# A planned two-layer decoder trunk: DeltaNet's gate projected with tokens as rows, memory accounted by single columns, the first gate bias loaded later

## The chip, the cores and the metric

The kernel runs on one core of a Trainium2 chip. The metric is the device time of one execution in microseconds, lower is better. Engines: PE (TensorE) with its weight loads PEld, DVE (VectorE), ACT (ScalarE), POOL (GpSimd), and SP, whose queue issues nearly all DMAs.

## What is computed

Two layers, each on x of 256 tokens by 1024 channels in fp32. One projection of the normalised x feeds three token mixers and three merge gates; the part that the change touches is the gate `za` of the first mixer, a gated delta rule with 4 heads of 128 (the reference, cut):

```python
def hybrid_layer(x, ...):
    h = rms_norm(x, norm_g)
    proj = jnp.einsum('btd,de->bte', h, w_in)
    (qa, ka, va, za, ba, aa, ub, zb, qc, kc, vc, zc, iq, ik, iw, gates) = split_columns(proj)
    ya = deltanet_branch(qa, ka, va, za, ba, aa, conv_w, a_log, dt_bias, dn_onorm)
    yb = pooling_branch(ub, zb, pool_w, pool_scale)
    yc = sparse_attention_branch(qc, kc, vc, zc, iq, ik, iw, ...)
    branches = jnp.stack([ya, yb, yc], axis=2)
    projected = jnp.einsum('btnc,ncd->btnd', branches, w_branch)
    gate = jax.nn.sigmoid(gates.reshape(b, t, N_BRANCH, D_MODEL) + gate_b)
    merged = jnp.sum(gate * projected, axis=2)
    return x + jnp.einsum('btd,de->bte', merged, w_out)

def deltanet_branch(...):
    ...
    o = chunk_gated_delta_rule(q, k, v, beta, g)
    o = rms_norm(o, o_norm) * jax.nn.silu(za.reshape(b, t, DN_HEADS, DN_DV))
    return o.reshape(b, t, DN_WIDTH)
```

## The kernel before

**Products.** Every large fp32 product is made of three matmuls on a rounded high part and the remainder as low part: high by high, high by low, low by high. A weight piece of 128 x 1024 comes by DMA into `raw` (4 buffers), ACT or DVE casts it to `wh` (6 buffers), and DVE subtracts to get `wl` (6 buffers); this is `wslot`. The activations are `hh` and `hl`, with channels on the partitions. `proj_cm` gives a result with channels as rows: for each block of 128 channels one weight piece, 24 matmuls of 256 columns (all tokens). `proj_tm` gives a result with tokens as rows: four weight pieces of 512 channels, held through two halves of 128 tokens, 24 matmuls of 512 columns each. PSUM banks are `pj` (4, projections) and `mx` (4, the rest).

**Scratch.** `u` (15 units of 512 columns), `f` (short-lived), `y` (fp32r operands of products), `big`, `tg` (merge gates and their biases), `z` (gates with channels as rows).

**The gate.** In DeltaNet's end the two token halves `o0`, `o1` are normalised, each is transposed by four PE transposes into an `mx` bank (`onT`), and these banks wait until `gated()`: it projects the gate with `zgate(ZA)` (two `proj_cm`, each followed by `silu2`, a tanh on ACT and one multiply on DVE), multiplies bank, scale `hb` and gate in one DVE instruction, and splits into `yah` and `yal`, the operands of the branch's output product.

**The order.** The program is written down once as a list of operations; the class `Plan` then orders them. `lay_out` is a list scheduler: it keeps a simulated time for each engine, holds operations that are ready, and picks by priority or by a deadline (`late`) that `deadlines` works out from the pass before; of 6 passes the best is kept. Its inputs are the prices in `cost`, `SWITCH` (what it charges PE for going from whole-array to small matmuls or back), the operations' earliest times `plan.begin`, and the dependences. These it finds from memory: `Ref.mask` gives the columns that an operand touches as a bit mask, in groups of four columns, and two operands with a common bit, one of them written, depend on each other. `emit` (L542) then issues everything in the order found, so every instruction in the profile has line L542, and rows are told apart by tile names. The order on each engine is fixed; the waits between engines are real.

**Stages, by time.** Load and normalise x, then k, v and the index projections of sparse attention (to about 57 us); its scores and top-k, DeltaNet's convolutions, the pooling mixer (57-190); the inverse of DeltaNet's triangular matrix in 32 x 32 blocks at 190, then its recurrence, the gate, branch products and output (190-320); the same for layer 1 (320-458, 458-576). The pooled channels go through a small product per group (`mx<-y,wl`), and k is transposed per head into `mx` banks, from which ACT takes sums of squares (`ssk`) and scaled copies.

Of the kernel before, what the change touches and what calls it, by code (L numbers as in the profile page):

```python
# [42 lines left out]
KOUT = 4  # L43
NWARM = 40

SWITCH = 90.0

REST = 2500.0

# [39 lines left out]
class Ref:  # L89
# [25 lines left out]
    def mask(self):  # L115
        (width, _), *free = self.ap.ap
        key = (self.ap.offset % width, tuple(free))
        got = self.tile.tag.masks.get(key)
        if got is None:
            idx = np.array([key[0]])  # L120
            for step, num in free:
                if step:
                    idx = (idx[:, None] + step * np.arange(num)[None, :]).reshape(-1)
            got = 0
            for g in np.unique(idx // 4):
                got |= 1 << int(g)
            self.tile.tag.masks[key] = got
        return got

# [54 lines left out]
class Plan:  # L184
# [35 lines left out]
    def cost(self, eng, call, args, kw):  # L220
# [28 lines left out]
            return hold + (120 if acc else 0), (95 if ps else 22) + (90 if acc else 0), False  # L249
        if eng == "POOL":  # L250
            if kw.get("op") == ALU.pow:
                return 400.0 + 155 * n, 240.0, False
            if call == "memset":
                return 50 + 0.8 * n, 50.0, False
            return 90 + 2.2 * w, 60.0, True
# [291 lines left out]
def trunk(ctx: ExitStack, tc: tile.TileContext, x, norm_g, w_in, gate_b, conv_w, a_log, dt_bias, dn_onorm,  # L547
# [32 lines left out]
    def unit(tag="u"):  # L580
        return make(tag, [128, 512])

    def fill():
        return make("f", [128, 512])
# [7 lines left out]
    def bank(tag):  # L592
        return plan.tile(tags[tag], [128, 512])

    def v4(t):
        return t.rearrange("p (h d) -> p h d", h=4)
# [123 lines left out]
    for l in range(DEPTH):  # L720
# [551 lines left out]
        V.tensor_tensor(o1, four(hsl(aT[1]), w1), qs, op=ALU.add)  # L1272


        onT = []
        for c, o in ((0, o0), (1, o1)):
            so, se, ro = small(4, "so"), small(4, "so2"), small(4, "so3")
            sumsq(o, so, unit())
            V.tensor_scalar(se, ssq[:, 4 * c:4 * c + 4], 4 * EPS, 128 * EPS, op0=ALU.add, op1=ALU.mult)
            V.scalar_tensor_tensor(se, so, 1.0 / 128, se, op0=ALU.mult, op1=ALU.add)  # L1280
            rsqrt(ro, se)
            V.tensor_tensor(v4(o), v4(o), ro[:, :, None].to_broadcast([128, 4, 128]), op=ALU.mult)
            ps = bank("mx")
            for h in range(4):
                PE.transpose(ps[:, h * 128:(h + 1) * 128], o[:, h * 128:(h + 1) * 128], ident)
            onT.append(ps)

        def gated():
            za = zgate(ZA)
            for c, ps in enumerate(onT):  # L1290
                y = unit()
                cc = slice(c * 128, (c + 1) * 128)
                V.scalar_tensor_tensor(v4(y), v4(ps), hb[:, 4:5], za[:, :, cc], op0=ALU.mult, op1=ALU.mult)
                split(v4(y), yah[:, :, cc], yal[:, :, cc])


        acc = [big()[:, :D] for _ in range(2)]
# [15 lines left out]
        for n, (i, yh, yl) in enumerate(((1, ybh, ybl), (2, ych, ycl), (0, yah, yal))):  # L1313
            wb = w_branch[l, i].rearrange("(k p) n -> p k n", p=128)
            gates = []
            if n == 2:
                gated()
            for half in range(2):
                cols = slice(half * 512, (half + 1) * 512)
                bias = make("tg", [128, 512], F32)  # L1320
                spread(DMA, bias, gate_b[l, i, cols])
                banks = by_token(wi[:, :, GT + i * D + half * 512:GT + i * D + (half + 1) * 512], KB, (hh, hl))
                tg = [make("tg", [128, 512], F32), bias]
                for t in range(2):
                    V.tensor_tensor(tg[t], banks[t], bias, op=ALU.add)
                    S.activation(tg[t], tg[t], AF.Tanh, scale=0.5)
                gates.append(tg)
            for half, tg in enumerate(gates):
                cols = slice(half * 512, (half + 1) * 512)
                banks = by_token(wb[:, :, cols], 4, (yh, yl))  # L1330
                for t in range(2):
                    at = acc[t][:, cols]
                    if n == 0:
                        V.scalar_tensor_tensor(at, tg[t], 1.0, banks[t], op0=ALU.add, op1=ALU.mult)
                        continue
                    V.scalar_tensor_tensor(tg[t], tg[t], 1.0, banks[t], op0=ALU.add, op1=ALU.mult)
                    V.tensor_tensor(at, at, tg[t], op=ALU.add)
                    if n == 2:
                        ps = bank("mx")
                        for k in range(4):  # L1340
                            c0 = half * 512 + k * 128
                            PE.transpose(ps[:, k * 128:(k + 1) * 128], acc[t][:, c0:c0 + 128], ident)
                        dst = [z[half][:, :, t * 128:(t + 1) * 128] for z in (mh, ml)]
                        S.activation(dst[0], v4(ps), AF.Copy, scale=0.5)
                        V.scalar_tensor_tensor(dst[1], v4(ps), 0.5, dst[0].bitcast(F32), op0=ALU.mult,
                                               op1=ALU.subtract)
# [63 lines left out]
```

## Time and profile before

| | us |
|---|---|
| median of 3 runs | 578.9 (578.34 to 580.63) |
| the profiled execution, its own time | 578.55 |
| its span, first to last instruction | 576.4 |
| PE busy | 566.5 |
| DVE busy | 484.8 |
| ACT busy | 297.0 |
| POOL busy | 35.6 |

The span is what the timelines cover; some 2 us of the execution lie outside it. An engine is busy while an instruction of its own runs; PE's matmuls are pipelined, so the pace is read from the distance between starts, not from the mean duration of one. In timelines a bracket gives the idle time before a row and the instruction that ended it.

### The profile page before, as it was taken

Reading aid. Unit: us, or ns where it says so; the run is one execution under the profiler, and the core shown is the slowest. Engines: PE = TensorE matmul, PEld = TensorE weight load, DVE = VectorE, ACT = ScalarE, POOL = GpSimd, SP = SyncE. Lnnn points to the kernel's source line nnn. Section 1 sums busy time; section 2 is a strip of 40 time slices with the busy share of each in tenths; the row PEclk is TensorE's granted clock in tenths of the full one; section 3 lists DMA queues with packets and bytes.
Section 4 is the critical chain, followed back from the end, with each engine's and each line's share of the span. In section 5 each row is a group of like instructions: output and inputs, shape, how many; then the busy total and the mean of one; then the engine's idle time right before and its main releaser. Section 6 shows DMA issues by size and latency. Waiting matters only on the chain.

```text
span 576.4 us, 10225 instructions
## 1 busy us (share of the span) xinstructions
PE 566.5 (98%) x3846; PEld 504.1 (87%) x3846; DVE 484.8 (84%) x1026; ACT 297.0 (52%) x574; POOL 35.6 (6%) x47
## 2 busy tenths in 40 slices
PE   8999999999999999999999999999999999999997
PEld 7887999998888789988879889999998878898886
DVE  5996999999999759658599999999999966766672
ACT  6754646756463452544346645776464534445520
POOL 4400000000100001000011002000100010000000
PEclk9999999999999999999999999999999999999999
DMA  9875458545766743565526559457457644666511
GB/s 309 266 209 163 112 145 235 134 144 167 228 182 211 202 129 110 183 216 186 181 64 215 148 140 257 112 150 202 137 160 231 205 141 113 178 193 207 177 38 73
DMA packets 95937, 98.71 MB, mean 171 GB/s; under 512 B 5616, under 2 KB 66848, under 8 KB 95888
## 3 DMA queue, kind: packets, MB, share of 16 engines
q1 hardware_dynamic: 95328, 97.47, 57.0%
q0 software_dynamic: 560, 0.60, 0.4%
q8 instruction: 30, 0.49, 0.4%
q14 instruction: 19, 0.16, 0.1%
HBM read 97.00 MB, written 1.05 MB: 170 GB/s over the span
## 4 chain that ended last, share of the span: by engine, by line
PE 82%; DVE 11%; issue 2%; ACT 2%; DMA 2%; POOL 1%; SPq 0%; DVEq 0%; ACTq 0%; POOLq 0%
PE pj L542 64%; PE mx L542 18%; DVE wl L542 4%; DVE u L542 3%; DVE big L542 1%; DMA x_sb<-in_x_dram 1%; DMA raw<-in_w_in_dram 1%; POOL r4k L542 1%; ACT u L542 1%; ACT wh L542 0%; DVE hl L542 0%; DVE y L542 0%; DVE tg L542 0%; POOL rk L542 0%; DVE wh L542 0%
## 5 line engine op out<-in xcount | busy, mean ns | idle before, releaser
L542 ACT CAST wh<-raw 128x1024 fp32r<-128x1024 f32 (+1 forms) x164 | 171.5, 1048 | 169.3 <-PE pj L542 117.8
L542 DVE TENSOR_TENSOR wl<-raw,wh 128x1024 fp32r<-128x1024 f32 (+1 forms) x174 | 211.1, 1220 | 32.4 <-ACT wh L542 26.8
L542 PE MATMUL pj<-wh,hh 128*128 128x512 f32 (+1 forms) x320 | 91.0, 388 | 0.9 <-ACT hh L542 0.9
L542 PE MATMUL pj<-wh,hl 128*128 128x512 f32 (+1 forms) x320 | 90.0, 386 | 1.1 <-DVE hl L542 1.1
L542 PE MATMUL pj<-wl,hh 128*128 128x512 f32 (+1 forms) x320 | 90.2, 385 | 0.0
L542 PEld LDWEIGHTS pj<-wh,hl 128*128 128x128 f32 x320 | 59.1, 188 | 13.0 <-DVE hl L542 2.0
L542 PEld LDWEIGHTS pj<-wh,hh 128*128 128x128 f32 x320 | 58.6, 188 | 11.9 <-ACT hh L542 1.3
L542 PEld LDWEIGHTS pj<-wl,hh 128*128 128x128 f32 x320 | 58.8, 188 | 10.7
L542 PE MATMUL pj<-hh,wh 128*128 128x256 f32 x448 | 64.4, 285 | 0.3 <-ACT wh L542 0.3
L542 PE MATMUL pj<-hl,wh 128*128 128x256 f32 x448 | 64.3, 284 | 0.0
L542 PE MATMUL pj<-hh,wl 128*128 128x256 f32 x448 | 63.6, 284 | 0.0
L542 PEld LDWEIGHTS pj<-hh,wh 128*128 128x128 f32 x448 | 58.3, 192 | 0.8 <-ACT wh L542 0.5
L542 PEld LDWEIGHTS pj<-hl,wh 128*128 128x128 f32 x448 | 58.1, 192 | 0.0
L542 PEld LDWEIGHTS pj<-hh,wl 128*128 128x128 f32 x448 | 58.0, 192 | 0.0
L542 PE MATMUL pj<-wh,y 128*128 128x512 f32 (+1 forms) x208 | 51.9, 384 | 0.0
L542 PEld LDWEIGHTS pj<-wh,y 128*128 128x128 f32 x208 | 38.3, 188 | 7.4
L542 PE MATMUL mx<-wh,y 128*128 128x512 f32 (+1 forms) x128 | 38.1, 380 | 0.0
L542 PEld LDWEIGHTS mx<-u,u 128*128 128x128 f32 (+2 forms) x336 | 31.2, 165 | 2.9 <-issue 2.1
L542 PE MATMUL mx<-u,u 128*128 128x128 f32 (+2 forms) x336 | 32.6, 249 | 0.0
L542 DVE SCALAR_TENSOR_TENSOR u<-pj,pt,u 128x255 f32<-128x255 f32 (+2 forms) x72 | 29.8, 480 | 0.0
L542 PE MATMUL pj<-wl,y 128*128 128x512 f32 (+1 forms) x104 | 29.2, 386 | 0.0
L542 PEld LDWEIGHTS mx<-wh,y 128*128 128x128 f32 x128 | 23.4, 188 | 4.4 <-DVE y L542 0.2
(206 smaller groups left out, 665.7 us busy)
## 6 DMA issues: line engine op xcount, KB each, us to landing
raw<-in_w_in_dram SPq DMA_DIRECT2D x128, 512.0 KB, 3.9
raw<-in_w_branch_dram SPq DMA_DIRECT2D x24, 512.0 KB, 3.4
raw<-in_w_out_dram SPq DMA_DIRECT2D x16, 512.0 KB, 3.3
tg<-in_gate_b_dram SPq DMA_DIRECT2D x12, 256.0 KB, 4.3
raw<-in_w_in_dram SPq DMA_DIRECT2D x4, 486.0 KB, 4.9
x_sb<-in_x_dram SPq DMA_DIRECT2D x2, 512.0 KB, 4.2
out_dram<-x_sb SPq DMA_DIRECT2D x3, 256.0 KB, 2.0
raw<-in_w_in_dram SPq DMA_DIRECT2D x2, 324.0 KB, 3.7
```

The lines of the kernel that those rows point to most:

```text
L542: getattr(self.real[o.eng], o.call)(*[put(a) for a in o.args], **{k: put(v) for k, v in o.kw.items()})
```

## The change

Five edits.

- The planner's price of a switch goes from 90 to 160 ns.
- `Ref.mask` marks single columns, not groups of four. Operands that lie in one group of four but share no column no longer depend on each other in the plan.
- The planner's price of POOL's power goes from 400 + 155n, with 240 until the result is seen, to 405 + 151n and 10.
- The DMAs of the gate biases may not be planned before 25 us (of the planner's time). This moves the first of them.
- DeltaNet's gate is projected by `proj_tm`. Each token half of `o` is multiplied by its gate while tokens are still rows, then transposed, and the scale `hb` is applied in two instructions that read the bank: ACT's copy makes the high part, one DVE instruction the low part.

```diff
-SWITCH = 90.0
+SWITCH = 160.0
...
-            got = 0
-            for g in np.unique(idx // 4):
-                got |= 1 << int(g)
+            bits = np.zeros(int(idx.max()) // 8 * 8 + 8, np.uint8)
+            bits[idx] = 1
+            got = int.from_bytes(np.packbits(bits, bitorder="little").tobytes(), "little")
...
             if kw.get("op") == ALU.pow:
-                return 400.0 + 155 * n, 240.0, False
+                return 405.0 + 151 * n, 10.0, False
...
-            ps = bank("mx")
-            for h in range(4):
-                PE.transpose(ps[:, h * 128:(h + 1) * 128], o[:, h * 128:(h + 1) * 128], ident)
-            onT.append(ps)

         def gated():
-            za = zgate(ZA)
-            for c, ps in enumerate(onT):
-                y = unit()
+            for c, (o, ps) in enumerate(zip((o0, o1), proj_tm(ZA))):
+                za = fill()
+                silu2(ps, za, "f")
+                V.tensor_tensor(o, o, za, op=ALU.mult)
+                ps = bank("mx")
+                for h in range(4):
+                    PE.transpose(ps[:, h * 128:(h + 1) * 128], o[:, h * 128:(h + 1) * 128], ident)
                 cc = slice(c * 128, (c + 1) * 128)
-                V.scalar_tensor_tensor(v4(y), v4(ps), hb[:, 4:5], za[:, :, cc], op0=ALU.mult, op1=ALU.mult)
-                split(v4(y), yah[:, :, cc], yal[:, :, cc])
+                S.activation(yah[:, :, cc], v4(ps), AF.Copy, scale=hb[:, 4:5])
+                V.scalar_tensor_tensor(yal[:, :, cc], v4(ps), hb[:, 4:5], yah[:, :, cc].bitcast(F32), op0=ALU.mult,
+                                       op1=ALU.subtract)
...
                 bias = make("tg", [128, 512], F32)
+                plan.begin = 25000.0
                 spread(DMA, bias, gate_b[l, i, cols])
+                plan.begin = 0.0
```

Where the plan puts things then differs in many places; three of them follow, as the order of instructions of one engine, before and after.

PE in layer 1 at DeltaNet's gate: `pj` banks, `hh` and `hl` the normalised x, `cs` the identity in a transpose. Before:

```order
L542 MATMUL pj_118<-hh_79,wh_68 128x256 x8
L542 MATMUL pj_118<-hl_80,wh_68 128x256 x8
L542 MATMUL pj_118<-hh_79,wl_73 128x256 x8
L542 MATMUL pj_118<-hh_79,wh_69 128x256 x8
L542 MATMUL pj_118<-hl_80,wh_69 128x256 x8
L542 MATMUL pj_118<-hh_79,wl_74 128x256 x8
L542 MATMUL pj_115<-hh_79,wh_70 128x256 x8
L542 MATMUL pj_115<-hl_80,wh_70 128x256 x8
```

After:

```order
L542 MATMUL pj_115<-wl_73,hh_79 128x512 x2
L542 MATMUL pj_115<-wh_69,hh_79 128x512 x2
L542 MATMUL pj_115<-wh_69,hl_80 128x512 x2
L542 MATMUL pj_115<-wl_74,hh_79 128x512 x2
L542 MATMUL pj_115<-wh_70,hh_79 128x512 x2
L542 MATMUL pj_115<-wh_70,hl_80 128x512 x2
L542 MATMUL pj_115<-wl_75,hh_79 128x512 x2
L542 MATMUL pj_115<-wh_71,hh_79 128x512 x2
L542 MATMUL pj_115<-wh_71,hl_80 128x512 x2
L542 MATMUL pj_115<-wl_76,hh_79 128x512 x2
L542 MATMUL mx_122<-cs_124,u_99 128x128 x4
```

The eight rows before are 64 matmuls of 256 columns with a weight slot each 24; after, two matmuls for each half-slot of 512 columns, the second half (`pj_115`) reading the same slots as the first, and then the first half's four transposes (`mx_122<-cs_124`).

ACT in layer 0 between the casts of weight pieces: the first rows `ACTIVATE u,ssk<-mx` are the sums of squares of k's transposes, `ACTIVATE u<-mx,eg` the scaled copies of the same bank. Before:

```order
L542 CAST y_83<-big_112 128x256 x2
L542 CAST y_83<-big_114 128x256 x2
L542 CAST wh_69<-raw_66 128x1024
L542 ACTIVATE u_110,ssk_189<-mx_120 128x128 x2
L542 CAST wh_70<-raw_63 128x1024
L542 ACTIVATE u_110,ssk_189<-mx_120 128x128
L542 ACTIVATE u_98<-mx_120,eg_180 128x128
L542 ACTIVATE u_110,ssk_189<-mx_120 128x128
L542 ACTIVATE u_98<-mx_120,eg_180 128x128 x3
```

After:

```order
L542 CAST wh_70<-raw_65 128x1024
L542 COPY big_113<-pj_115 128x2x256
L542 CAST wh_71<-raw_66 128x1024
L542 CAST wl_78<-u_109 128x512
L542 ACTIVATE u_102,ssk_189<-mx_122 128x128 x4
L542 ACTIVATE u_110<-mx_122,eg_180 128x128 x4
L542 CAST wh_72<-raw_63 128x1024
L542 ACTIVATE u_109<-u_107 128x512
```

Before, casts of pooled channels (`y<-big`) and weight casts stand ahead of the sums of squares and one weight cast stands between them; after, all eight rows of the bank stand together, ahead of the cast of `wh_72`.

PE in layer 1 where the inverse begins: `u,um` with 32x32 is its first product, rows with `y` a branch product, rows with `hh` a projection. Before:

```order
L542 MATMUL pj_117<-wh_67,y_84 128x512
L542 MATMUL pj_116<-wh_67,y_84 128x512
L542 MATMUL pj_117<-wh_67,y_84 128x512
L542 MATMUL pj_116<-wh_67,y_84 128x512
L542 MATMUL pj_117<-wl_78,y_83 128x512
L542 MATMUL pj_116<-wl_78,y_83 128x512
L542 MATMUL pj_117<-wl_78,y_83 128x512
L542 MATMUL pj_116<-wl_78,y_83 128x512
L542 MATMUL pj_118<-wh_68,hh_79 128x512
L542 MATMUL pj_115<-wh_68,hh_79 128x512
L542 MATMUL mx_122<-u_97,um_136 32x32 x32
```

After:

```order
L542 MATMUL pj_116<-wh_72,y_83 128x512
L542 MATMUL pj_118<-wh_72,y_83 128x512
L542 MATMUL pj_116<-wh_72,y_83 128x512
L542 MATMUL pj_118<-wh_72,y_83 128x512
L542 MATMUL mx_122<-u_105,um_136 32x32 x32
L542 MATMUL pj_116<-wh_72,y_84 128x512
L542 MATMUL pj_118<-wh_72,y_84 128x512
L542 MATMUL pj_116<-wh_72,y_84 128x512
L542 MATMUL pj_118<-wh_72,y_84 128x512
```

The first 32x32 product now stands ahead of the branch product's `y_84` rows of one weight slot and of the whole next slot, 22 matmuls of 512 columns earlier.

## Rows read from the trace of the kernel before

**Rows 1.** The page's first section (busy time of each engine, us, share of the span, instructions), from its second section the granted clock in tenths and the GB/s of the 40 slices, and the first line of its fourth section, the chain that ended last by engine.

```profile
PE 566.5 (98%) x3846; PEld 504.1 (87%) x3846; DVE 484.8 (84%) x1026; ACT 297.0 (52%) x574; POOL 35.6 (6%) x47
...
PEclk9999999999999999999999999999999999999999
...
GB/s 309 266 209 163 112 145 235 134 144 167 228 182 211 202 129 110 183 216 186 181 64 215 148 140 257 112 150 202 137 160 231 205 141 113 178 193 207 177 38 73
...
PE 82%; DVE 11%; issue 2%; ACT 2%; DMA 2%; POOL 1%; SPq 0%; DVEq 0%; ACTq 0%; POOLq 0%
```

**Rows 2.** Busy time by stage, whole kernel after the start: stretch and its length in us, then busy us and instruction count of each engine, the granted clock, the DMA share and GB/s.

```profile
57.00:190.00 133.00, 131.37 (x911) 122.13 (x911) 130.22 (x327) 77.75 (x155) 5.33 (x5) 1.00 0.60 174
190.00:320.00 130.00, 129.14 (x897) 109.73 (x896) 98.97 (x145) 61.59 (x115) 6.17 (x7) 1.00 0.55 165
320.00:458.00 138.00, 137.88 (x944) 128.24 (x943) 136.36 (x351) 80.09 (x161) 5.24 (x5) 1.00 0.61 171
458.00:576.40 118.40, 115.21 (x826) 98.27 (x824) 74.03 (x100) 44.95 (x69) 4.60 (x4) 0.99 0.46 144
```

**Rows 3.** PE's timeline at its gaps: start us, us, engine, line, operation, tiles and shape, count, and in brackets the idle time before and what ended it.

```profile
10.44 0.76 PE L542 MATMUL pj<-wh,hh 128*128 128x512 f32 x2 [0.88 <-ACT hh L542]
11.69 0.76 PE L542 MATMUL pj<-wh,hl 128*128 128x512 f32 x2 [0.49 <-DVE hl L542]
...
27.68 0.55 PE L542 MATMUL mx<-cs,u 128*128 128x128 f32 x3 [0.54 <-DVE u L542]
...
142.88 0.98 PE L542 MATMUL mx<-y,wl 128*128 128x256 f32 x6 [1.25 <-ACT u L542]
...
190.69 0.74 PE L542 MATMUL mx<-u,um 32*32 32x32 f32 x64 [0.29 <-DVE u L542]
```

**Rows 4.** PE's timeline where it runs without a gap, at 256 columns (128 us) and at 512 (188 us); the pace is the distance of two starts over the count.

```profile
128.57 1.12 PE L542 MATMUL pj<-hl,wh 128*128 128x256 f32 x8
129.53 1.12 PE L542 MATMUL pj<-hh,wl 128*128 128x256 f32 x8
...
188.19 1.07 PE L542 MATMUL pj<-wl,hh 128*128 128x512 f32 x4
189.10 1.07 PE L542 MATMUL pj<-wh,hh 128*128 128x512 f32 x4
```

**Rows 5.** Groups of instructions by operation, tiles and shape over the whole kernel: count, then busy us and mean ns of one, then idle us before them and what ended it.

```profile
L542 DVE TENSOR_TENSOR wl<-raw,wh 128x1024 fp32r<-128x1024 f32 x168 | 204.8, 1225 | 32.4 <-ACT wh L542 26.8 <-issue 4.0 <-PE pj L542 0.7
...
L542 PE MATMUL mx<-cs,u 128*128 128x128 f32 x88 | 13.1, 274 | 0.5 <-DVE u L542 0.5
...
L542 DVE TENSOR_TENSOR y<-u,y 128x512 fp32r<-128x512 f32 x16 | 10.7, 686 | 0.0
...
L542 ACT CAST y<-u 128x512 fp32r<-128x512 f32 x15 | 9.2, 620 | 1.0 <-DVE u L542 0.7
...
L542 DVE SCALAR_TENSOR_TENSOR z<-f,pj 128x512 f32<-128x512 f32 x12 | 8.2, 683 | 0.0
...
L542 DVE CAST wh<-raw 128x1024 fp32r<-128x1024 f32 x10 | 6.8, 688 | 3.0 <-PE mx L542 2.5 <-PE pj L542 0.5
...
L542 DVE SCALAR_TENSOR_TENSOR y<-mx,y 128x512 fp32r<-128x512 f32 x8 | 5.3, 689 | 3.3 <-ACT y L542 3.3
L542 DVE SCALAR_TENSOR_TENSOR big<-tg,pj 128x512 f32<-128x512 f32 x8 | 5.3, 678 | 0.0
...
L542 ACT ACTIVATE y<-mx 128x512 fp32r<-128x512 f32 x8 | 4.6, 597 | 8.4 <-PE mx L542 8.3
...
L542 DVE COPY u<-mx 128x512 f32<-128x512 f32 x5 | 3.4, 689 | 1.8 <-PE mx L542 1.7
...
L542 DVE SCALAR_TENSOR_TENSOR u<-mx,hb,z 128x512 f32<-128x512 f32 x4 | 2.8, 747 | 0.1
```

**Rows 6.** DVE's timeline in 211-234, layer 0, around the place where DeltaNet's gate is projected: two of the rows that begin after idle time.

```profile
215.26 0.69 DVE L542 SCALAR_TENSOR_TENSOR tg<-tg,pj 128x512 f32<-128x512 f32 x1 [2.86 <-PE pj L542]
...
231.31 1.23 DVE L542 TENSOR_TENSOR wl<-raw,wh 128x1024 fp32r<-128x1024 f32 x1 [1.16 <-ACT wh L542]
```

**Rows 7.** Timelines of DVE, ACT, POOL and DVE again in the first 27 us.

```profile
6.51 1.22 DVE L542 TENSOR_TENSOR wl<-raw,wh 128x1024 fp32r<-128x1024 f32 x1 [1.36 <-ACT wh L542]
...
15.27 1.03 ACT L542 CAST wh<-raw 128x996 fp32r<-128x996 f32 x1 [1.97 <-DMA raw<-in_w_in_dram]
...
23.06 3.84 POOL L542 TENSOR_TENSOR r4k<-se,mhalf 128x4 f32<-128x4 f32 x1 [5.75 <-DVE se L542]
...
26.93 0.69 DVE L542 TENSOR_TENSOR u<-u,r4k 128x512 f32<-128x512 f32 x1 [0.94 <-POOL r4k L542]
```

**Rows 8.** The view of one tile name, tg (the gates): DVE's sums of a gate's projection and its bias, duration ns min/median/max, then first and last start in us.

```profile
L542 DVE TENSOR_TENSOR tg<-pj,tg x24: 653/686/694, 154.9 to 539.9; 128x512 f32<-128x512 f32 x24
```

**Rows 9.** ACT's timeline in 135-144, layer 0: a weight cast and the first of the sums of squares behind it.

```profile
140.22 1.05 ACT L542 CAST wh<-raw 128x1024 fp32r<-128x1024 f32 x1 [1.10 <-DMA raw<-in_w_in_dram]
141.18 0.27 ACT L542 ACTIVATE u<-mx 128x128 f32<-128x128 f32 x1
```

**Rows 10.** DVE's timeline in 138-144, layer 0: the row after its idle time.

```profile
142.09 0.17 DVE L542 TENSOR_SCALAR ssk<-ssk 128x4 f32<-128x4 f32 x1 [0.72 <-ACT u L542]
```

**Rows 11.** Timelines of DVE (457.85, the last step before the inverse's blocks) and of PE (458.67, their first product) in layer 1.

```profile
457.85 0.45 DVE L542 STREAM_TRANSPOSE u<-xi 128x256 f32<-128x256 f32 x1
...
458.67 0.75 PE L542 MATMUL mx<-u,um 32*32 32x32 f32 x64
```

More of the change, by code (lines that the diff above doesn't have):

```diff
@@ L1272, in trunk @@
         V.tensor_tensor(o1, four(hsl(aT[1]), w1), qs, op=ALU.add)
-        onT = []
         for c, o in ((0, o0), (1, o1)):
```

## The prediction

> **What bounds the kernel now.** I read the page's first and fourth sections first [rows 1]: TensorE is busy for 566.5 of 576.4 us, and the chain that ended last lies on PE for 82% and on DVE for 11%. PE is the bound, so a change can gain in two ways only: less PE work, or fewer of the short gaps between PE's instructions. The clock row stands at 9 in every slice, the full 2.4 GHz, so the pace of the matmuls has nothing to give. Next the busy time by stage [rows 2]: DVE is saturated in 57-190 (130.22 of 133.00) and in 320-458 (136.36 of 138.00), and has room in the rest (98.97 of 130, 74.03 of 118.4). Each saturated stretch ends at the inverse of DeltaNet's triangular matrix; there PE waits for DVE, or nearly. Then PE's own gaps [rows 3]: 0.88 us at 10.44 and 0.49 at 11.69 in the start, 0.54 before the transposes of k at 27.68, 1.25 at 142.88, 0.29 at 190.69. Together these are 3.45 us, the most that a better order could win at these places.
>
> **Part 1: the gate's projection.** Channels as rows takes 192 matmuls of 256 columns in the two layers, tokens as rows 96 of 512. That is the same number of columns. A run of 512 costs 0.910 us for 4 (188.19 to 189.10), so 0.2275 each, and a run of 256 0.96 for 8, so 0.120 each [rows 4]. Removed 192 x 0.120 = 23.04, added 96 x 0.2275 = 21.84: **-1.2 us**, all on PE and so on the path. The Trainium skill's page "TensorE: Matmul & The Clock Gate", section "Back-to-back issue gap", gives a warm gap of N/2.4 + 2.5 ns, 109 and 216 ns; by it this term would be 0.25 us instead of 1.2, and the forecast 578.1. The trace disagrees with it at both widths (120 and 227.5 ns), and the trace decides.
>
> The elementwise work keeps its count. Per token half go a gated multiply from PSUM (683 ns), a second one with the scale (747), the low half's subtraction (686) on DVE and a cast on ACT (620); in come one from PSUM (683), a multiply in SBUF (no such row; nearest is that subtraction, 686), ACT's scaled copy (no such row with a scale at this width; nearest its activation y<-mx at 597, and at the other end DVE's product with such a scale, 747) and the subtraction from PSUM (689) [rows 5]. DVE loses 0.06 us per half, which is nothing.
>
> What is new is a chain between projection and product: tanh 0.60 (as the activation above), multiply 0.68, multiply 0.69, four transposes at 0.15 (13.1 us busy for 88 of that form), copy 0.60, subtraction 0.69, or 3.9 us [rows 5]. In the new order the product that reads it stands 78 matmuls after the transposes, 78 x 0.2275 = 17.7 us, and the transposes stand a whole 24-matmul half (5.5 us) behind the first half's bank. Cover: 17.7 against the 1.9 us from the transposes on. The projection holds all its four weight slots through both halves, so their pieces are wanted every 1.36 us (6 x 0.2275) in place of every 2.88 (24 x 0.120). DVE has spare time there (2.86 us idle at 215.26, 1.16 at 231.31) [rows 6]. PE idles only 0.86 of the 130 us in that stretch [rows 2], so ACT and DVE lead it there. I put 0 here; if that cover failed, a late piece would cost one subtraction, 1.2 us, per layer.
>
> **Part 2: the start.** The first gate bias (256 KB) leaves the queue ahead of the fifth raw piece; ACT waits 1.97 us for that piece at 15.27 [rows 7]. At the 309 GB/s of the first slice [rows 1] the bias takes 0.85 us (estimate), the most that the piece can gain. The new order also normalises the low half of x ahead of the first weight subtraction (1.22 us at 6.51), and finishes the first token half's low channels before the next cast. Against it the second token half's scaling comes after one more subtraction (1.2 us). The bias moves behind four more pieces in SP's queue; its first reader starts at 154.9 [rows 8], so nobody waits for it. The transposes of k, which wait behind POOL's r4k (3.84 us, then 0.69 on DVE), stand 14 matmuls of 332 columns (2.1 us, an estimate at 332/512 of 0.2275 each) earlier; the sum of squares that r4k needs now stands ahead of a product, a half-width pair and a weight subtraction on DVE, some 2.4 us earlier (estimate from rows of their kinds) [rows 5], so that wait stays about as it is. Bounds: +1.2 (that subtraction alone) to -1.4 (the gaps at 10.44 and 11.69 gone). I take **-0.3**, near zero because the chain from x to the first product keeps all its links.
>
> **Part 3: layer 0's product of the pooled channels (1.25 us at 142.88).** It waits for a bank that ACT still reads: the sums of squares of k's transposes stand behind a weight cast that waited 1.10 us for its DMA and took 1.05 [rows 9]. In the new order ACT does these reads ahead of the later casts, and the two products use banks that others left long before. This gap of 1.25 goes. But what follows is DVE's inverse chain, and DVE is saturated. Ahead of its end, DVE loses a weight cast (0.69), a cast of half the size (0.34) and one of two 512-column copies (0.69), and gains another copy of that width (0.69) [rows 5]: 1.0 us. Its 0.72 us of idle at 142.09 [rows 10], which the same bank caused, may go too. So the first 32x32 product can start 1.0 to 1.7 us earlier. It stands three 512-column matmuls (0.68 us) earlier in PE's order, which is no gain, as that work comes after it. Net -0.35 to -1.05; I take **-0.65**. PE will wait there 1.25 + 0.29 less that net, 0.5 to 1.2 us, in place of 0.29: most of the gap has moved. If the start's gain reaches PE but not DVE, it ends in this wait too.
>
> **Part 4: layer 1's inverse chain.** Its first 32x32 product stands 22 matmuls earlier, 5.0 us. Before, DVE ended its transpose at 458.30 and PE began at 458.67 [rows 11], 0.37 us of slack. From the last top-k preparation to this transpose DVE does 3 weight subtractions (3.67), 2 copies (1.39) and 2 merges big<-tg,pj (1.36) less, and casts that all but cancel: 6.1 us less; counted from the first top-k step, 2 subtractions less and some small steps of the top-k more, 4.3 us less [rows 5]. DVE was busy throughout, so its chain ends 4.3 to 6.1 us earlier against 5.0 - 0.37 = 4.6 needed: a wait of 0 to 0.3, up to 1.0 with scatter. I take **+0.3**. The work put off, wl and merges, falls into 458-576, where DVE has 44 us of room [rows 2].
>
> **Part 5: the rest.** The planner's prices for a switch and for POOL's power cost the chip nothing by themselves, and 24 changes between whole and small matmuls stay 24. New banks and units may be wanted a little early, +0.1. The other small gaps of PE keep their neighbours in the order.
>
> Sum against the profiled execution, which took 578.55 us in all: 578.55 - 1.2 - 0.3 - 0.65 + 0.3 + 0.1 = 576.8. That execution lies 0.35 below the median of 578.9, so the forecast for the median is **577.1 us**; its own range is 575.7 to 578.7.
>
> **Rivals.** *Slower: layer 1's product gets ahead of DVE.* If DVE's chain is not earlier (because what was dropped from it only makes it wait for PE's top-k scores or ACT), PE stands still for 5.0 - 0.37 = 4.6 us at this one place. It decides as soon as DVE's transpose is less than 2.3 us earlier, where the gains are used up. For it speaks that PE's order is fixed and DVE's count is from an order, not from times; against it that DVE was never idle there. Time 577.1 - 0.3 + 4.6 = 581.4, with layer 0's part also lost 582.0.
>
> *Faster: the gaps really go.* If DVE's chain in layer 0 follows fully (1.25 + 0.29), the start gives 1.1 and k's transposes 0.5: -1.2 - 1.1 - 1.54 - 0.5 = -4.3, so 578.9 - 4.3 = 574.6. For it: every one of these gaps has a named cause that the new order touches. Against: behind each stands a saturated DVE.
>
> *No change: the plan merely shuffles.* The 1.2 us of PE stay, but new waits of the same size come where the order differs: slots wanted twice as fast in both layers at 1.2 us a miss, or the start at +1.2. Time 578.3 to 579.5.
>
> **How the numbers follow.** Chances: forecast 0.45, no change 0.22, faster 0.22, slower 0.11. A measurement of this kernel can tell about 0.5% (2.9 us) from no change, so faster means under 576.0 and slower over 581.8. Faster by over 0.5% takes the faster case and 0.08 of the forecast's lower end, 0.30; slower takes the slower case and 0.02 of the shuffle's tail, 0.13; 0.57 remain. The range leaves out the slower case and a tail of the faster one: 574.2 to 580.8.
>
> **What would show it.** PE's rows for the gate read x2 of 512 columns, with PE's busy time about 1.2 us shorter. ACT no longer waits 1.97 us for the fifth piece. The row of 142.88 has no idle, and the first 32x32 product in layer 0 shows 0.5 to 1.5 us of idle, released by DVE; in layer 1 it shows under 1 us. DVE has less idle in 57-190. Wrong would be: over 2 us at layer 1's product; gaps in PE's rows with wl or wh as releaser inside the gate's projection; a first product later than 10.44.

## The result and the profile after

The changed kernel takes 575.98 us (median of 6 runs, 575.6 to 576.62) against 578.86 for the kernel before in the same comparison (578.22 to 580.63): ratio 0.9943, 95% interval 0.9928 to 0.9958, 2.9 us faster. The forecast was 577.1 in a range of 574.2 to 580.8; the result also lies just past the 576.0 from which the prediction counts it as faster, an outcome that it gave a chance of 0.30. A second comparison gave 575.92 against 578.74, ratio 0.9949 (0.9935 to 0.9962). The first profiled execution took 576.62 us, the slowest of its six, with a span of 574.5; the second profile has a span of 573.7.

The page of the changed kernel, in the order of [rows 1]: busy times, clock, and the chain that ended last.

```profile
PE 565.3 (98%) x3750; PEld 498.8 (87%) x3750; DVE 483.8 (84%) x1021; ACT 299.5 (52%) x579; POOL 33.4 (6%) x47
...
PEclk9999999999999999999999999999999999999999
...
PE 73%; DVE 19%; DMA 3%; issue 3%; ACT 2%; SPq 0%; POOL 0%; DVEq 0%; ACTq 0%
```

PE lost 1.2 us of busy time (566.5 to 565.3) and the chain shifted: DVE's share rose from 11% to 19%, PE's fell from 82% to 73%. That is the first sign that PE got ahead and waits for DVE at more places. The stages, with the columns of [rows 2]:

```profile
57.00:190.00 133.00, 131.56 (x973) 122.55 (x972) 130.79 (x328) 79.00 (x154) 5.29 (x5) 1.00 0.60 175
190.00:320.00 130.00, 129.53 (x795) 108.50 (x794) 99.82 (x157) 61.70 (x116) 7.84 (x8) 1.00 0.55 169
320.00:458.00 138.00, 136.64 (x1057) 126.38 (x1056) 135.39 (x337) 79.27 (x159) 5.74 (x6) 1.00 0.60 167
458.00:574.50 116.50, 113.28 (x652) 95.00 (x650) 72.16 (x94) 45.33 (x70) 2.49 (x3) 1.00 0.45 143
```

PE now idles 1.36 us of 138 in 320-458, where it idled 0.12. PE's timeline at its gaps, to be held against [rows 3]:

```profile
9.75 0.63 PE L542 MATMUL pj<-wh,hh 128*128 128x512 f32 x2
10.22 0.62 PE L542 MATMUL pj<-wh,hl 128*128 128x512 f32 x2
...
14.60 0.61 PE L542 MATMUL pj<-wh,hl 128*128 128x512 f32 x2
15.36 0.73 PE L542 MATMUL pj<-wl,hh 128*128 128x512 f32 x2
...
24.64 0.60 PE L542 MATMUL mx<-cs,u 128*128 128x128 f32 x4
...
54.36 0.74 PE L542 MATMUL mx<-kiT,qiT 128*128 128x128 f32 x4 [0.87 <-ACT kiT L542]
...
83.20 0.63 PE L542 MATMUL mx<-cs,big 128*128 128x128 f32 x4 [0.40 <-DVE big L542]
...
188.25 0.74 PE L542 MATMUL mx<-u,um 32*32 32x32 f32 x64 [1.00 <-DVE u L542]
...
297.19 1.09 PE L542 MATMUL mx<-cs,big 128*128 128x128 f32 x8 [0.42 <-ACT big L542]
...
362.46 0.63 PE L542 MATMUL mx<-cs,big 128*128 128x128 f32 x4 [0.66 <-ACT big L542]
...
452.42 0.75 PE L542 MATMUL mx<-u,um 32*32 32x32 f32 x64 [0.70 <-DVE u L542]
```

The first projection starts at 9.75 in place of 10.44, and its second row follows without the gap that stood at 11.69. The transposes of k (24.64) no longer wait. At 142.88 there is no row with a gap any more. The wait before layer 0's first 32x32 product has grown from 0.29 to 1.00 us; new are 0.70 before layer 1's and waits of 0.40 to 0.66 for `big` at 83.20, 297.19 and 362.46. The one at 297.19, at the passage from layer 0 to layer 1 (called the seam below), takes the place of one that the rows of before do not show:

```profile
295.31 0.74 PE L542 MATMUL pj<-wh,hl 128*128 128x512 f32 x2 [0.56 <-DVE hl L542]
```

The unchanged gap of layer 0's first index product (0.87 at 54.36; 0.86 at 55.37 before) serves as a mark of time.

Four marks split the 576.4 us of before and the spans of the two profiles after:

| mark, us | before | after | after, again |
|---|---|---|---|
| first index product, layer 0 | 55.37 | 54.36 | 54.00 |
| first 32x32 product, layer 0 | 190.69 | 188.25 | 188.00 |
| first 32x32 product, layer 1 | 458.67 | 452.42 | 451.63 |
| end of the span | 576.4 | 574.5 | 573.7 |

PE's work ahead of a mark changed too: 0.68 us less stands ahead of layer 0's 32x32 product and follows it, and 22 matmuls (5.0 us) less stand ahead of layer 1's. With this taken out, the start gave 1.0 and 1.4 us (first and second profile), layer 0 up to its inverse 0.75 and 0.64, the stretch from there to layer 1's inverse gave 0.6 by its gate and lost 1.1 and 0.6, and the rest gave 0.6 and 0.7. The sums are 1.9 and 2.7 us. Each profile is one execution, and the two, of the same program, differ by 0.8 us.

The gate of layer 0 on PE's timeline, first and last rows and the transposes behind them:

```profile
222.59 0.61 PE L542 MATMUL pj<-wh,hh 128*128 128x512 f32 x2
223.04 0.62 PE L542 MATMUL pj<-wh,hl 128*128 128x512 f32 x2
...
233.02 0.62 PE L542 MATMUL pj<-wl,hh 128*128 128x512 f32 x2
233.48 0.60 PE L542 MATMUL mx<-cs,u 128*128 128x128 f32 x4
```

48 matmuls from 222.59 to 233.48 are 10.89 us, 0.227 each, with no wait for a weight in between; 96 of 256 columns take 11.52 at the 0.120 of [rows 4].

### The profile page after: what moved, and what is told of

It reads as the page before. It is cut to its first block, busy times and chain, and to the rows that moved or that the text cites. A ratio compares the mean times of both kernels' runs of the same rounds, so it can differ in the third digit from the quotient of the medians.

```text
span 574.5 us, 10043 instructions
## 1 busy us (share of the span) xinstructions
PE 565.3 (98%) x3750; PEld 498.8 (87%) x3750; DVE 483.8 (84%) x1021; ACT 299.5 (52%) x579; POOL 33.4 (6%) x47
## 4 chain that ended last, share of the span: by engine, by line
PE 73%; DVE 19%; DMA 3%; issue 3%; ACT 2%; SPq 0%; POOL 0%; DVEq 0%; ACTq 0%
PE pj L542 57%; PE mx L542 16%; DVE wl L542 7%; DVE u L542 4%; DMA raw<-in_w_in_dram 2%; DVE big L542 2%; DVE score L542 2%; DMA x_sb<-in_x_dram 1%; DVE top L542 1%; DVE hl L542 1%; ACT big L542 1%; DVE mxm L542 0%; ACT u L542 0%; DVE tg L542 0%; ACT wh L542 0%
## 5 line engine op out<-in xcount | busy, mean ns | idle before, releaser
L542 ACT CAST wh<-raw 128x1024 fp32r<-128x1024 f32 (+2 forms) x164 | 172.1, 1051 | 150.1 <-PE pj L542 102.8
L542 PE MATMUL pj<-wh,hh 128*128 128x512 f32 (+1 forms) x352 | 100.4, 388 | 0.1
L542 PE MATMUL pj<-wl,hh 128*128 128x512 f32 (+1 forms) x352 | 100.2, 387 | 0.1
L542 PE MATMUL pj<-wh,hl 128*128 128x512 f32 (+1 forms) x352 | 99.6, 385 | 0.1
L542 PE MATMUL pj<-hh,wh 128*128 128x256 f32 x384 | 55.6, 284 | 0.0
L542 PE MATMUL pj<-hl,wh 128*128 128x256 f32 x384 | 55.3, 284 | 0.0
L542 PE MATMUL pj<-hh,wl 128*128 128x256 f32 x384 | 54.7, 283 | 0.0
L542 PEld LDWEIGHTS pj<-hh,wh 128*128 128x128 f32 x384 | 50.0, 191 | 0.2
L542 PEld LDWEIGHTS pj<-hl,wh 128*128 128x128 f32 x384 | 49.9, 192 | 0.0
L542 PEld LDWEIGHTS pj<-hh,wl 128*128 128x128 f32 x384 | 49.8, 192 | 0.0
```

The costliest lines, as they stand in the source:

```text
L542: getattr(self.real[o.eng], o.call)(*[put(a) for a in o.args], **{k: put(v) for k, v in o.kw.items()})
```

## The experiments

**Parts by the plan.** Five kernels take single edits out of the change or put them into the kernel before; the planner then draws the plan anew. The edits are the hunks of the diff above and are not repeated in full.

*The gate alone.*

```diff
 (kernel before)
-            za = zgate(ZA)
+            for c, (o, ps) in enumerate(zip((o0, o1), proj_tm(ZA))):
...
```

> The kernel before with the new gate alone (projection with tokens as rows, product before the transposes); until the first layer's gate PE's order is the old one. Columns theory: each layer's gate projection takes 48 matmuls at 0.2275 us in place of 96 at 0.120, 0.6 us less, no new gap on PE inside it: about 1.2 us below the kernel before, 577.7. Rival, weight slots wanted twice as fast: gaps on PE with wh or wl as releaser inside the projection, up to 1.2 us each layer, so 578 to 580.

Measured 577.52 us against 579.22, ratio 0.9962 (0.9949 to 0.9974). PE's rows at the two inverses:

```profile
190.80 0.74 PE L542 MATMUL mx<-u,um 32*32 32x32 f32 x64 [0.28 <-DVE u L542]
...
458.21 0.75 PE L542 MATMUL mx<-u,um 32*32 32x32 f32 x64
```

Before they stood at 190.69 and 458.67, so 0.57 us went between them; the span ended at 575.3, which is 117.1 behind the second mark in place of 117.7. That is 0.6 in each layer, as the columns theory has it, and no gap on PE names a weight inside the projection. The ratio's interval (1.5 to 3.0 us) begins a little above this; the runs of before on this chip ranged from 578.39 to 580.48, and the trace gives 1.1.

*Everything but the gate.*

```diff
 (changed kernel)
-            for c, (o, ps) in enumerate(zip((o0, o1), proj_tm(ZA))):
+            za = zgate(ZA)
...
```

> The changed kernel with the old gate; up to the gate of layer 0 PE's order is the changed one. Theory of separate parts: PE reaches the first 32x32 product of layer 0 as early as in the changed kernel (about 188.2 us) and the whole is 1.2 us slower than it, about 577.2. Rival, the gain hangs on the gate's new order as a whole: back to 578.9.

Measured 577.14, ratio 0.9956 (0.9944 to 0.9969). The changed kernel's two ratios are 0.0007 and 0.0013 lower, 0.4 to 0.8 us, which is less than the intervals can tell; the 1.2 us between 577.14 and 575.92 compares different chips. The traces show more. PE's row at layer 0's inverse:

```profile
187.53 0.74 PE L542 MATMUL mx<-u,um 32*32 32x32 f32 x64 [0.39 <-DVE u L542]
```

It comes 0.7 and 0.5 us earlier than in the two profiles of the changed kernel, though up to the gate of layer 0 every engine's order is the same in both kernels. Behind this row, where the gates lie, the changed kernel is 1.0 and 1.6 us faster by its marks. So the gate's columns and the new order add up as two separate parts, about 1.2 and about 2 us.

*The later bias alone.*

```diff
 (kernel before)
+                plan.begin = 25000.0
                 spread(DMA, bias, gate_b[l, i, cols])
+                plan.begin = 0.0
```

> The kernel before with the later gate bias alone; PE's order changes by 16 rows, all in the start. Theory, the start's gain of 1.0 us (kiT product at 54.36 in place of 55.37) comes from the order in which x's low half is normalised and split, not from the bias: ACT's wait for the fifth piece falls from 1.97 us to 1.1 to 1.4, but PE's gaps of 0.88 and 0.49 stay and the whole gains 0 to 0.3 us. Rival, the bias held the start up: gaps gone or nearly, kiT product at 54.4, 577.9 in all.

Measured 578.66, ratio 0.9988 (0.9979 to 0.9997). That is 0.2 to 1.2 us faster by the interval, 0.4 by the profile's span (576.0). Neither theory fits by itself, since the new plan did more than move the bias: it exchanged the first weight piece and a table in SP's queue. PE's start:

```profile
7.49 0.19 PE L542 MATMUL mx<-cs,u 8*128 8x8 f32 x1 [1.53 <-DMA u<-in_norm_g_dram]
...
10.72 0.63 PE L542 MATMUL pj<-wh,hh 128*128 128x512 f32 x2
11.19 0.61 PE L542 MATMUL pj<-wh,hl 128*128 128x512 f32 x2
...
55.26 0.74 PE L542 MATMUL mx<-kiT,qiT 128*128 128x128 f32 x4 [0.86 <-ACT kiT L542]
```

The gap of 11.69 is gone, but the first projection is 0.28 us later than before and the mark at 55 stands at 55.26. What was won in one place was lost in the load before it.

*The account by single columns, alone and taken out.*

```diff
 (kernel before; in the second kernel the changed one, the other way round)
-            for g in np.unique(idx // 4):
-                got |= 1 << int(g)
+            bits[idx] = 1
...
```

> The kernel before with memory accounted by single columns alone; the whole plan is drawn anew. If the new orders of the start and of layer 0 come from this account: the first projection near 9.7, no gap at 142.88, about 2 us faster, 576.9. If they come from the prices or are chance: gaps like those of before in other places, 578 to 580.

> The changed kernel with memory accounted by groups of four columns again. If the account carries the new orders: only the gate's 1.2 us and the start's part remain, 577.2 to 577.7. If it does not: 576.0 as the changed kernel.

Alone it gave 579.02, ratio 1.0004 (0.9994 to 1.0013), no change. Without it the changed kernel takes 575.43, ratio 0.9940 (0.9928 to 0.9953), as fast as with it. So the gain does not need the account; the gate with the two prices and the bias gives it too, by another order. Which of the two prices matters was not tried, nor how far the chance of a newly drawn plan goes. In the plan without the account layer 1's first 32x32 product stands 20 matmuls later than in the changed kernel; it starts at 455.31 without a wait, and the stretch between the two inverses loses nothing where the changed kernel loses 1.1 and 0.6 us. The run with the account alone shows why a won start need not count. Its rows at the two marks of layer 0:

```profile
53.75 0.74 PE L542 MATMUL mx<-kiT,qiT 128*128 128x128 f32 x4 [0.86 <-ACT kiT L542]
...
191.76 0.74 PE L542 MATMUL mx<-u,um 32*32 32x32 f32 x64 [1.38 <-DVE u L542]
```

It is 1.62 us ahead at the first mark (53.75 for 55.37) and then stands for 1.38 us before the inverse, waiting for DVE. Seven more matmuls of 512 columns (1.6 us) stand ahead of this inverse than before; with that and the like behind it taken out, the stretch up to the inverse lost 1.1 us and the rest of the kernel 1.0.

**Parts in a fixed order.** The next kernels keep the plan of one kernel, instruction by instruction, and move a few of them:

```diff
-        for o in self.plan():
+        order = list(self.plan())
+        at = {}
+        for o in order:
+            at.setdefault(o.eng, []).append(o)
+        for e, first, last, behind in MOVES:
+            group, after = at[e][first:last + 1], at[e][behind]
+            order = [o for o in order if o not in group]
+            i = order.index(after) + 1
+            order[i:i] = group
+        for o in order:
```

*The bias by itself, in the order of before.*

```diff
+MOVES = [("SP", 10, 10, 20)]
```

> The kernel before in its own order, with one DMA moved: the first gate bias leaves SP's queue behind the piece with which it stands in the changed kernel (row 21 in place of 11), nothing else. The run with the later bias alone also exchanged the first raw piece and a table in the queue, so it did not show the bias by itself. Theory, the bias holds nobody on PE: ACT's wait at 15.27 falls from 1.97 to 1.1 to 1.4 us, PE's gaps at 10.44, 11.69 and 27.68 stay, kiT's product stays at 55.4, no change (within 0.3 us). Rival, the earlier fifth piece carries through: PE up to 0.85 us earlier at 55, 578.0.

Measured 578.59, ratio 0.9999 (0.9985 to 1.0014). ACT's row for the fifth piece, and PE's mark:

```profile
14.15 1.03 ACT L553 CAST wh<-raw 128x996 fp32r<-128x996 f32 x1 [0.69 <-DMA raw<-in_w_in_dram]
...
55.42 0.74 PE L553 MATMUL mx<-kiT,qiT 128*128 128x128 f32 x4 [0.86 <-ACT kiT L553]
```

ACT casts the piece 1.12 us earlier (14.15 for 15.27 in [rows 7]) and waits 0.69 instead of 1.97, yet PE's mark stays. The bias held ACT up and nobody behind it.

*ACT's reads ahead of one cast, in the order of before.*

```diff
+MOVES = [("ACT", 147, 147, 153)]
```

> The kernel before in its own order, but one cast of a weight piece on ACT (wh3, at 140.22) stands behind the sums of squares and scaled copies of k's transposes instead of between them. Theory, moved gap: the 1.25 us gap at 142.88 goes, DVE's 0.72 us idle at 142.09 goes with it, PE then waits 0.7 to 0.9 us in place of 0.29 at the first 32x32 product (190.69) and 0.6 to 0.75 us are gained in all, 578.2. Rival, DVE does not bound PE there: 1.25 us gained. Second rival, the bank's readers were not the cause: gap and time stay.

Measured 577.32, ratio 0.9957 (0.9944 to 0.9970). PE's rows at the product of 142.88 and at the inverses, and the busy times of the stretch 138-160 (columns as in [rows 2]), of the kernel before and then of this one:

```profile
141.56 0.88 PE L553 MATMUL mx<-y,wl 128*128 128x256 f32 x6
...
189.49 0.74 PE L553 MATMUL mx<-u,um 32*32 32x32 f32 x64 [0.28 <-DVE u L553]
...
457.46 0.75 PE L553 MATMUL mx<-u,um 32*32 32x32 f32 x64
```

```profile
138.00:160.00 22.00, 20.75 (x115) 17.55 (x115) 20.70 (x52) 12.83 (x30) 2.85 (x2) 1.00 0.68 221
```

```profile
138.00:160.00 22.00, 22.00 (x121) 18.54 (x120) 21.65 (x53) 13.52 (x34) 2.85 (x2) 1.00 0.70 226
```

The gap of 142.88 is gone, and the first 32x32 product comes 1.20 us earlier with the same 0.28 us of waiting. The moved-gap theory expected 0.7 to 0.9 us of waiting there and is refuted; the first rival holds, by the trace. The ratio's interval (1.7 to 3.2 us) lies above the trace's 1.2, as with the gate alone. DVE in 138-160 was busy for 20.70 us before and is for 21.65 in the same stretch here: what made PE's gap had held DVE up too, by 0.95 us and not only by the 0.72 at 142.09.

*The start of the changed kernel's kind, in the order of before.* The move table here also names the engine behind whose instruction a group goes.

```diff
+MOVES = [("PE", 39, 42, ("PE", 34)), ("DVE", 3, 3, ("DVE", 4)), ("ACT", 4, 7, ("ACT", 11)),
+         ("DVE", 10, 11, ("DVE", 15)), ("DVE", 7, 8, ("DVE", 15)), ("SP", 13, 14, ("DVE", 11))]
```

> The kernel before in its own order, with the start of the changed kernel's kind: DVE normalises the low half of x ahead of the first weight subtraction, PE transposes it right behind the high half, ACT and DVE make hh and hl of the low half ahead of the high half's and of the second weight piece; the bias stays where it was. Theory, the start's gain is this order: first projection at 9.3 to 9.8 in place of 10.44, the gap at 11.69 gone, kiT's product 0.7 to 1.4 us earlier and the whole 0.7 to 1.4 us faster, 577.6 to 578.2. Rival, the second half of x or POOL's r4k is late instead: the gap at 27.68 grows by what was won, kiT's product stays, 578.9. Second rival, won at 55 but swallowed at the first 32x32 product by DVE: its gap grows to over 1 us, 578.9.

Measured 581.34, ratio 1.0037 (1.0024 to 1.0049), slower. PE's start:

```profile
9.37 0.63 PE L553 MATMUL pj<-wh,hh 128*128 128x512 f32 x2
9.96 0.76 PE L553 MATMUL pj<-wh,hl 128*128 128x512 f32 x2
...
14.53 0.72 PE L553 MATMUL pj<-wl,hh 128*128 128x512 f32 x2 [2.05 <-DVE wl L553]
...
17.45 0.77 PE L553 MATMUL mx<-cs,big 128*128 128x128 f32 x5 [0.58 <-DVE big L553]
```

The first projection starts at 9.37, 1.07 us earlier than before, and the gap of 11.69 is gone: this part is the order in which the low half is made. But the same moves put the second weight subtraction behind seven of DVE's eight `hl` steps, and DVE waits 1.80 us among them (up to 12.47) for an `hh` that ACT makes behind two casts; PE waits 2.05 us for the subtraction at 14.53 and 0.58 for `big` at 17.45. At layer 0's first index product the kernel is 1.06 us late (56.43). The changed kernel puts this subtraction after five of the eight `hl` steps and has no gap of its size there; it loses 0.3 us at 15.36 (0.76 from 14.60 for two matmuls in place of 0.455), at its fourth weight piece. So the run shows where the first gain comes from and where it can be lost; what the changed start as a whole is worth is read from the marks, not from this run.

**Versions beyond the change.** Three kernels keep the changed kernel's order and attack its new gaps; the changed kernel itself ran beside them.

> The changed kernel once more, for its gaps and to stand on the same chip as the three that follow. The same gaps on PE as in its first profile, 0.8 to 1.1 us at the first 32x32 products of both layers, released by DVE; about 576.0.

Its time was 575.92 as expected, its gaps both outside the 0.8 to 1.1:

```profile
188.00 0.74 PE L542 MATMUL mx<-u,um 32*32 32x32 f32 x64 [1.24 <-DVE u L542]
...
451.63 0.75 PE L542 MATMUL mx<-u,um 32*32 32x32 f32 x64 [0.33 <-DVE u L542]
```

The expectations that follow count the waits of the first profile as 1.07 and 0.77 us, by the distance of starts.

*DVE's chain ahead of a weight subtraction.*

```diff
+MOVES = [("DVE", 392, 394, 390), ("DVE", 840, 843, 838)]
```

> The changed kernel in its own order, but in each layer the last three steps of DVE's inverse chain (two scalings and the transpose) stand ahead of the weight subtraction that comes before them. Theory, DVE's chain sets PE's wait at the first 32x32 product: the waits of 1.07 and 0.77 us shrink by up to the 1.13 us that a subtraction takes, to nothing, 1.5 to 1.8 us gained, 574.3. Rival, the wait is set by something else (a bank, ACT): waits and time stay at 576.0. Second rival, the subtraction is then late for PE: a new gap with wl as releaser behind it, 576.0 or more.

*PE's next matmuls ahead of the 32x32 products.*

```diff
+MOVES = [("PE", 1182, 1186, 1149), ("PE", 2774, 2777, 2741)]
```

> The changed kernel in its own order, but on PE the next five (layer 0) and four (layer 1) 512-column matmuls stand ahead of the first 32x32 products instead of behind them. Theory, PE has other work ready while DVE's chain ends, so both waits are filled: 1.07 and 0.77 us gained, 574.2. Rival, what follows the inverse runs later by the same amount and PE waits further on: 576.0.

The first gives 574.48, ratio 0.9924 (0.9912 to 0.9936), the second 574.65, ratio 0.9926 (0.9914 to 0.9938); both spans end at 572.1, 1.6 us below the changed kernel beside them. PE's rows, the first kernel's and then the second's:

```profile
186.67 0.75 PE L553 MATMUL mx<-u,um 32*32 32x32 f32 x64
...
450.01 0.75 PE L553 MATMUL mx<-u,um 32*32 32x32 f32 x64
```

```profile
187.88 0.75 PE L553 MATMUL mx<-u,um 32*32 32x32 f32 x64
...
450.91 0.75 PE L553 MATMUL mx<-u,um 32*32 32x32 f32 x64
```

No row has idle time. The two waits of 1.24 + 0.33 us are what the spans gained, by either way; the medians gained 1.4 and 1.3. DVE's chain does set these waits, and PE has other work that can stand there. (The first kernel moves three of DVE's steps in layer 0 and four in layer 1.)

*Four more gaps.*

```diff
+MOVES = [("PE", 1182, 1186, 1149), ("PE", 2774, 2777, 2741), ("PE", 472, 476, 467),
+         ("PE", 1740, 1742, 1731), ("PE", 2122, 2127, 2117), ("PE", 258, 260, 253)]
```

> As the run with both gaps filled, and four more of PE's gaps in the changed kernel: five 256-column matmuls ahead of the transposes at 83.2, three 512-column ones ahead of those at 297.2, six 256-column ones ahead of those at 362.5, and the index keys' transposes ahead of four others at 53.0. If every gap is a short wait for a late operand with other work ready: a further 0.5 + 0.5 + 0.7 + 0.4 us, 572.1. If in the stretches where DVE is saturated the gap comes back at the next operand that DVE makes: only the seam's 0.5 us and the start's, 573.5 to 574.

Measured 574.63, ratio 0.9924 (0.9912 to 0.9936): nothing over the kernel with two gaps filled. The gaps at 83.2, 297.2 and 362.5 are gone, but the index keys' move made its own gap larger:

```profile
54.18 0.74 PE L553 MATMUL mx<-kiT,qiT 128*128 128x128 f32 x4 [1.19 <-ACT kiT L553]
```

1.19 us in place of 0.86. It begins layer 0's inverse 0.18 us later than the kernel with two gaps filled (188.06 and 187.88) and layer 1's at the same time (450.85 and 450.91). So of the gaps closed between the two inverses (0.45 and 0.46 us in that kernel) 0.2 was won, and what the gap at 83.2 held does not show at the first. That is the second guess of the expectation, and of the seam's 0.5 us, which it kept, at most half came.

## Why the prediction was right, and where it missed

The median came 1.1 us below the forecast, inside the range. Against the prediction's sum of -1.75 us for the profiled execution the spans fell by 1.9 and 2.7 us in the two profiles after. In the first, two misses cancel: the start gave 0.7 more than forecast and layer 1's stretch lost 0.8 more, so that the sum comes out there is luck. In the second the start gave 1.1 more and layer 1 lost 0.3 more.

**Part 1, the gate: right in mechanism and size.** Forecast -1.2; 0.6 in each layer by the rows of the gate alone, 10.89 us for layer 0's projection. The cover held: no gap names a weight or the gate's chain. The trace does not bear out the gap that the Trainium skill gives in "TensorE: Matmul & The Clock Gate", section "Back-to-back issue gap", for isolated matmuls, by which the term would have been 0.25.

**Part 2, the start: the step that was mis-sized.** Forecast -0.3, measured -1.0 and -1.4. The prediction saw that the low half is made earlier and had the right bound (-1.4), but took a value near zero because the chain from x to the first product keeps its links. That reason left out the order of the links on ACT and DVE: before, the low half's `hh` stood behind three of the high half's and a cast. The marks of the changed kernel show the gain, and the first rows of the run with the low half first show its first part by itself; no run shows the whole start alone. The wait at 27.68, which was to stay as it is (0.54 us), went too. POOL's `r4k` starts 2.42 us earlier, as estimated, and then takes 1.04 us where it took 3.84 before:

```profile
20.64 1.04 POOL L542 TENSOR_TENSOR r4k<-se,mhalf 128x4 f32<-128x4 f32 x1 [3.31 <-DVE se L542]
```

Why it took longer in the order of before (3.84 and 2.70 in profiles with that order) stays open. That the bias is worth nothing to PE was right in the sum; it went behind ten pieces and not four, and nobody waited for it there either.

**Part 3, layer 0's gap: the sum right (forecast -0.65, measured -0.75 and -0.64), the reason for it only in part.** The predicted wait of 0.5 to 1.2 us came too (1.00 and 1.24). But "most of the gap has moved" is refuted for the gap alone: taken out of the kernel before, it gave its whole 1.20 us. That DVE is busy 98% of a stretch does not tell that its chain would have ended at the same time: in that run about 1.0 of the 2.8 us that DVE idled in 57-190 went with the gap. This 1.2 and the 1.0 us of work that DVE lost in the new order could have brought its chain 2.2 us earlier; with the start's gain taken out it came 1.4 and 1.3. What took the rest shows in DVE's timeline:

```profile
151.19 1.23 DVE L542 TENSOR_TENSOR wl<-raw,wh 128x1024 fp32r<-128x1024 f32 x1 [0.60 <-ACT wh L542]
...
153.51 1.23 DVE L542 TENSOR_TENSOR wl<-raw,wh 128x1024 fp32r<-128x1024 f32 x1 [0.49 <-ACT wh L542]
```

and ACT's, which it waits for:

```profile
150.10 1.06 ACT L542 CAST wh<-raw 128x1024 fp32r<-128x1024 f32 x1 [1.31 <-DMA raw<-in_w_in_dram]
...
152.42 1.05 ACT L542 CAST wh<-raw 128x1024 fp32r<-128x1024 f32 x1 [0.74 <-DMA raw<-in_w_in_dram]
```

DVE waits 0.60 and 0.49 us for casts, and these 1.31 and 0.74 us for their weight pieces. So about as much as the 1.0 us of work that DVE lost went into waiting for pieces. This differs from one execution to the next: with the same order up to here, DVE waits in all 1.09 and 1.01 us in the two profiles of the changed kernel, but 0.52 without the gate (where the inverse began at 187.53), 0.53 and 0.51 in the two kernels that take away the inverses' waits. SP issues the later of the two pieces at nearly the same time in all five (146.10 to 146.41); its cast starts 5.9 to 6.0 us after that in the first two and 5.3 to 5.5 in the others. So the difference arises between issue and use and not in waiting for a buffer; what makes a piece slower there stays open.

**Part 4, layer 1: right mechanism, too small.** Forecast +0.3 with a bound of 1.0 for the product itself; it waits 0.70 and 0.33, and with the wait for `big` at 362.46 (0.66, and 0.49 in the second profile) the stretch lost 1.1 and 0.6. The gap at 362.46 is new, though PE's other small gaps were to stay as they are. The rival that the product would get ahead of DVE by 4.6 us did not come. DVE's last step before this product in the changed kernel:

```profile
451.92 0.45 DVE L542 STREAM_TRANSPOSE u<-xi 128x256 f32<-128x256 f32 x1
```

It starts 5.9 us earlier than before (457.85), and 6.7 in the second profile. About 2 us of this was won further up, which leaves some 4 for the steps that DVE dropped, the lower end of the 4.3 to 6.1 counted. (The rows named there for the upper end add up to 6.4.)

**Part 5: the seam.** The gap there went from `hl` (0.56 at 295.31 before) to `big` (0.42 at 297.19), about the same size. The 0.1 us set down for new waits is below what these profiles can tell.

**The rivals.** The slower one and the shuffle are refuted by the result; the faster one (574.6, all gaps gone) is the time that the two kernels with the filled inverses reach, 574.5 to 574.7, though some of the gaps are still there. The change itself does not reach it.

## What to carry to other kernels

Read an engine's share of 98% as a question, not as a bound: find its idle rows and who releases them, since the engine that it waits for may be the one that waits for it. Where two saturated engines meet at one product, the cheap gain is to let each run something else first: seven instructions of DVE or nine of PE moved past their neighbours gave 1.3 to 1.4 us on top of the change. And a gain at the start counts only as far as the first such meeting lets it through: the account by single columns won 1.6 us by 54 us, had lost 1.1 of it at the first inverse and had none of it at 576.

## What was not expected of the hardware

The same power on POOL over 128x4 took 3.84 us at one place of the kernel before and 1.04 in the changed one, and 1.0 to 1.5 in the other rows of its kind in both; no run here shows why. Profiles of one kernel differ by several tenths of a microsecond at the same place (1.00 and 1.24 us, 0.70 and 0.33 us before the two 32x32 products), so single gaps under about 0.4 us between two kernels are not evidence. That holds for the fifth piece too: its cast came 1.12 us earlier with the 256 KB bias out of its way, and the 0.85 that the bias's bytes come to at 309 GB/s (the prediction's estimate) is within that scatter.
